# Hybrid attention block on one core: third-order step in the norms, one ring for V, norm weights on the keys, shorter merges

## The chip, the cores and the metric

The kernel runs on one core of a Trainium2 chip. The metric is the device time of one execution in microseconds, the median of the runs. The engines are TensorE (PE in the profile, PEld its weight loads), VectorE (DVE), ScalarE (ACT), GpSimd (POOL) and SyncE (SP, which issues most of the DMAs). Each engine works through its own instructions in the order in which they were written, and waits for other engines by semaphores.

## The reference, cut to what matters

```python
h = rms_norm(x, norm_gain)                       # x: 2048 tokens x 1024, float32
proj = h @ w_in                                  # q, k, v of A and B, SiLU gates, merge gates
# mixer A: 8 query heads, 2 key heads of 64, window 128 to both sides, sink logit
qa = rms_norm(qa, q_norm_a) / 8;  ka = rms_norm(ka, k_norm_a)
ya = banded_attention(qa, ka, va, bias, sink) * silu(ga)
# mixer B: 3 groups of 8 heads, dilation 1, 4, 16, window 64 neighbours to both sides
qb = rms_norm(qb, q_norm_b) / 8;  kb = rms_norm(kb, k_norm_b)
outs, lses = [dilated_group(qb[g], kb[g], vb[g], dilation[g]) for g in range(3)]
alpha = softmax(lses, over g)
yb = sum(alpha[g] * outs[g]) * silu(gb)
merged = sigmoid(gate_a) * (ya @ w_branch_a) + sigmoid(gate_b) * (yb @ w_branch_b)
y = x + merged @ w_out
```

The norm of a head divides 64 values by the root of their mean square and multiplies them by a weight per position in the head. In a logit the weight of q and the weight of k stand in one product, position by position, so the kernel multiplies them together beforehand (`GT`, one row of 64 for A and one for B) and applies the product on one side only.

## The kernel before, in words

Every matrix product is made with float16 pairs: a value is split into a high and a low half, and three of the four products are summed, so that the result is near float32.

**Start (to about 57 us).** x is loaded in 16 tiles of 128 tokens, squared on ACT, scaled by the inverse root of its mean square, transposed on PE and split into XH and XL (`x_square`, `x_stats`, `x_newton`, `x_scale`, `x_turn`, `x_hi`, `x_lo`). Tiles 0, 1 and tiles 2, 3 have their root on DVE (lines 277 to 279), the later groups of four on POOL (lines 272 to 275). The products of the first two gate columns run on PE from there on.

**Units (to about 1380 us).** 14 units of 8 steps each: 2 units of A and, for each of 4 pairs of heads, the B groups with dilation 4, 16 and 1. A step handles one `Pair`, two subsets of 128 tokens. `Pair.matmuls` (line 655) makes q, k and v of a subset in 24 products of 384 columns into one of two PSUM tiles `pj`. Then, per pair: ACT copies q and k out (`evac_qk`, 673), ACT and DVE take V out as a high and a low half into a tile `vt` (`v_hi` 688, `v_lo` 694), ACT squares q and k (701), DVE sums the squares and makes a first guess of the inverse root (706, 707, 263), POOL improves the guess with three Newton rounds of four instructions (`rs_newton`, 272 to 275), DVE multiplies q and k by the root (`scale`, 718), POOL multiplies q by the norm weights (`gain`, 725, two instructions), ACT and DVE split into halves (`hi` 731, `lo` 735), POOL makes a copy of k with the halves swapped (`swap`, 740), and a DMA transposes the result into a ring `kq` (`turn`, 748). For the dilated groups ACT copies an edge of the ring (758, 760). A PSUM tile `pj` is free again only when `v_lo` has read it.

Some steps later the attention items of these subsets follow: logits on PE (833), bias and maximum on DVE (848), exponentials on ACT (856), halves (861, 865), a transposing DMA (871), and the product with V on PE (`values`, 882). The tile `vt` has one extra column per head that holds 2^-14, so that the product also gives the denominator. POOL writes that column for every subset (`v_ones`, 681) into a tile from a pool of ten buffers (`vt`), or of four (`vw`) for the first subset of a dilated class, which is used again at its end.

The units of dilation 1 also merge the three groups, once for 256 tokens (`b_merge_q`): DVE takes the minimum over the groups and the differences (1023 to 1025), ACT the exponentials (1028), DVE the factors (1031 to 1036), POOL three products (1041), DVE the two sums (1047, 1048); later PE transposes the result (944). In these units every step has one merge. Gate products (`g_step`, line 310) fill some of the steps as a third block of matrix products in the two `pj` tiles.

**Order.** All engines' orders come from one list of events by time in steps: `at(time, function)` puts an event in, `until` takes events out while the matrix products are written. The constants say when: for a pair that ends at e, `NORM` puts the nine stages from square to turn at e + 0.028 ... e + 1.118, `EVAC` the copies at e + 0.015, 0.025 and 0.099, and `V_ONES` the column of ones at e - 0.077. On each engine a later event stands behind an earlier one, whether or not it needs it. An example is DVE, where `v_lo` of a pair's second subset stands behind `lo` of the pair before:

```python
NORM = (0.028, 0.136, 0.32, 0.626, 0.744, 0.904, 0.962, 1.033, 1.118)
EVAC = (0.015, 0.025, 0.099)
at(e[i] - V_ONES, self.v_ones, i)
```

**Tail (from about 1380 us).** The merge gates, the branch products and the output product, on PE almost without a pause; the change doesn't touch them.

Of the kernel before, what the change touches and what calls it, by code (L numbers as in the profile page):

```python
# [61 lines left out]

V_ONES = 0.077
EVAC = (0.015, 0.025, 0.099)
# [42 lines left out]
KQ_COPY = 0.45  # L107
VT_BUFS = 10
PT_BUFS = 4
# [4 lines left out]
def block_kernel(tc, x, w_units, w_gate, w_mrg, w_brn, w_out, w_bra, gain, qkg, sink, bias_a, bias_b, b_merge, out):  # L114
# [151 lines left out]
    def rs_newton(a, yv, r, n, pool):  # L266

        t = sm.tile([128, 10], F32, name="rs_t")
        tv = t[:, :n]
        for i in range(3):  # L270
            if pool:
                G.tensor_tensor(tv, yv, yv, OP.mult)  # L272
                G.tensor_tensor(tv, tv, a, OP.mult)  # L273
                G.tensor_scalar(tv, tv, -0.5, 1.5, OP.mult, OP.add)  # L274
                G.tensor_tensor(r if i == 2 else yv, tv, yv, OP.mult)  # L275
                continue
            V.tensor_tensor(tv, yv, yv, OP.mult)
            V.scalar_tensor_tensor(tv, tv, -0.5, a, OP.mult, OP.mult)
            V.scalar_tensor_tensor(r if i == 2 else yv, tv, 1.5, yv, OP.add, OP.mult)

# [302 lines left out]
    class Unit:  # L583


        def __init__(self, u):
            self.kind, self.idx, self.g = UNITS[u]
            self.u = u
            assert ("w", u) in done
            self.wh, self.wl = wtiles[u][3:5]  # L590
            if self.kind == "A":
                self.nq, self.nk, self.nv = 4, 1, 1
                self.d, self.n = 1, NT
            else:
                self.nq, self.nk, self.nv = 2, 2, 2
                self.d = DIL[self.g]
                self.n = S // self.d // 128
            self.br = 0 if self.kind == "A" else 1
            self.shift = self.kind == "B" and self.n > 1
            self.v, self.kq, self.t, self.done = {}, {}, {}, {}  # L600
            if self.kind == "A" or self.g == 0:
                self.nm = us.tile([128, NT, self.nq], F32, name=f"nm{self.kind}", bufs=2)

        def scales(self):
# [5 lines left out]
            V.tensor_scalar(self.eps[:], self.eps[:], EPS * QKE, None, OP.mult)  # L610
            self.wsc = ucol()
            V.tensor_scalar(self.wsc[:], inv[:], 2.0 ** 6 / SX, None, OP.mult)
            ws[UNITS[self.u]] = self.wsc

# [21 lines left out]
    ring = wk.tile([128, 6, 2 * RING], F16, name="kq", bufs=1)  # L636
    blocks = [0]

    class Pair:
# [34 lines left out]

        def v_ones(self, i):
            un, nv = self.un, self.un.nv
            if un.shift and self.subsets[i][1] == 0:
                vt = wk.tile([128, 2, 130], F16, name="vw", bufs=4)
            else:
                vt = wk.tile([128, 2, 130], F16, name="vt", bufs=VT_BUFS)  # L680
            G.memset(vt[:, :nv, HD:HD + 1], 2.0 ** -14)  # L681
            self.vt[i] = vt

        def v_hi(self, i):
            w = self.nh * HD
            nv, vt = self.un.nv, self.vt[i]
            psv = self.ps[i][:, w:w + nv * HD].rearrange("p (h e) -> p h e", e=HD)
            A.activation(vt[:, :nv, 0:HD], psv, AF.Copy, scale=VSC)
            self.vt[i] = vt, psv
# [30 lines left out]
        def gain(self):  # L720
            un, n = self.un, 2 * self.nh
            q = self.rw[:, :n * HD].rearrange("p (s h e) -> p s h e", s=2, e=HD)
            g = GT[un.br][:].unsqueeze(1).to_broadcast([128, un.nq, HD])
            for i in range(2):
                G.tensor_tensor(q[:, i, :un.nq, :], q[:, i, :un.nq, :], g, OP.mult)  # L725

# [43 lines left out]
    class Item:  # L770
# [103 lines left out]
        def values(self):  # L874
# [3 lines left out]
            for j in range(2):  # L878
                vh = 0 if un.kind == "A" else j
                for k, (p, c0, w) in enumerate(((self.ph, 0, HD + 1), (self.ph, 66, HD), (self.pl, 0, HD + 1))):  # L880
                    for s, key in enumerate(self.segs):
                        T.matmul(self.po[:, j, :w], lhsT=p[:, n * j + s, :], rhs=un.v[key][:, vh, c0:c0 + w],  # L882
                                 start=(k == 0 and s == 0), stop=(k == 2 and s == n - 1))

        def z_load(self):
# [123 lines left out]
    def b_merge_q(t, un, zz, q):  # L1009

        j = un.idx
        wscs = [ws[("B", j, g)] for g in range(3)]
        nm = zz[:, :, :, :, 65]
# [8 lines left out]
        def exponents():  # L1022
            V.tensor_tensor(mn[:], nm[:, 0], nm[:, 1], OP.min)
            V.tensor_tensor(mn[:], mn[:], nm[:, 2], OP.min)
            V.tensor_tensor(e[:], mn[:].unsqueeze(1).to_broadcast([128, 3, 2, 2]), nm, OP.subtract)
# [4 lines left out]
        def factors():  # L1030
            V.tensor_tensor(ed[:], e[:], den, OP.mult)
            V.tensor_tensor(sd[:], ed[:, 0], ed[:, 1], OP.add)
            V.tensor_tensor(sd[:], sd[:], ed[:, 2], OP.add)
            V.reciprocal(sd[:], sd[:])
            for g in range(3):
                V.scalar_tensor_tensor(e[:, g], e[:, g], wscs[g][:], sd[:], OP.mult, OP.mult)

# [53 lines left out]

    ws, fill = {}, {}
    for u in range(NU + 1):
# [684 lines left out]
```

## Time and profile before

| what | value |
|---|---|
| median of 3 runs | 1948.53 us (1947.81 to 1949.16) |
| the profiled execution, its own time | 1949.46 us |
| its span, first to last instruction | 1947.7 us |
| mean granted TensorE clock | 0.996 |
| PE busy, instructions | 1923.5 us, 99%, 13702 |
| DVE busy | 1373.0 us, 70%, 3604 |
| ACT busy | 1073.4 us, 55%, 2451 |
| POOL busy | 953.4 us, 49%, 2440 |

How to read it: matrix products are pipelined. One of 384 columns is shown with some 0.33 us, but one starts every 0.16 us, so the profile's busy time of PE says little about its pace; the distance from start to start says it. When PE waits, the profile shows the idle time behind the modelled end of the product before, which is 0.16 us later than the moment at which the next one could have started.

### The profile page before, as it was taken

The numbers are of one execution on the slowest core, as the hardware profiler recorded it, in microseconds if no ns is written. First come the engines' busy times: TensorE is split into PE (matmuls) and PEld (weight loads), VectorE is DVE, ScalarE is ACT, GpSimd is POOL, SyncE is SP. The second block draws the span as 40 slices with busy tenths as digits, with TensorE's granted clock in tenths as the row PEclk, the third lists the DMA queues.
The fourth block names the chain that finished last, engine by engine and source line by source line (L and its number), as shares of the span: only waits on it lengthen the run. The fifth ranks groups of instructions, "written<-read, shape, count | busy, mean of one in ns | idle before, by whom it ended". The sixth has DMA issues, their size and how long they took to land.

```text
span 1947.7 us, 40273 instructions
## 1 busy us (share of the span) xinstructions
PE 1923.5 (99%) x13702; PEld 1211.9 (62%) x13702; DVE 1373.0 (70%) x3604; ACT 1073.4 (55%) x2451; POOL 953.4 (49%) x2440
## 2 busy tenths in 40 slices
PE   7999999999999999999999999999999999999999
PEld 5556676677766688566787567876544444444444
DVE  6668787888767776677876878768776756876422
ACT  7457666776565566665666656666534545422100
POOL 4254456445546756647666676656511310232533
PEclk8999999999999999999999999999999999999999
DMA  6239977797858596677767776765822246778763
GB/s 252 82 75 174 192 154 158 137 188 147 189 96 189 117 189 124 127 147 163 159 130 147 138 173 123 144 120 115 187 82 96 99 157 202 217 236 269 248 243 140
DMA packets 589743, 307.96 MB, mean 158 GB/s; under 512 B 458081, under 2 KB 527329, under 8 KB 588257
## 3 DMA queue, kind: packets, MB, share of 16 engines
q1 hardware_dynamic: 571104, 296.73, 64.7%
q10 hardware_dynamic: 18432, 8.66, 1.9%
q8 instruction: 107, 1.75, 0.4%
q14 instruction: 100, 0.81, 0.1%
HBM read 129.91 MB, written 65.27 MB: 100 GB/s over the span
## 4 chain that ended last, share of the span: by engine, by line
PE 49%; DVE 4%; POOL 3%; issue 2%; ACT 1%; DMA 1%; SPq 0%; DVEq 0%; POOLq 0%
PE pj L655 16%; PE fps L310 13%; PE fps L1645 7%; PE pj L310 6%; PE fps L1440 5%; PE s L833 1%; PE pv L882 1%; POOL rs_t L272 1%; POOL rs_t L273 1%; DVE rw L718 1%; DVE qss L706 1%; POOL rs_t L274 1%; DMA kq<-spl 0%; POOL rs_y L275 0%; DVE pr L848 0%
## 5 line engine op out<-in xcount | busy, mean ns | idle before, releaser
L655 PE MATMUL pj<-wh,XH 128*128 128x384 f16 x1792 | 584.7, 326 | 6.2 <-DVE vt L694 6.2
L655 PE MATMUL pj<-wh,XL 128*128 128x384 f16 x1792 | 586.6, 327 | 0.0
L655 PE MATMUL pj<-wl,XH 128*128 128x384 f16 x1792 | 585.2, 327 | 0.0
L655 PEld LDWEIGHTS <-XH 128*128 128x128 f16 x3584 | 412.9, 117 | 155.1 <-issue 8.1
L848 DVE CUSTOM_DVE_ANT_0 pr<-s,b,ubuf 128x256 f32<-128x256 f32 (+3 forms) x512 | 218.4, 463 | 51.3 <-PE s L833 49.9
L655 PEld LDWEIGHTS <-XL 128*128 128x128 f16 x1792 | 207.8, 116 | 68.8 <-issue 0.2
L272 POOL TENSOR_TENSOR rs_t<-rs_y 128x8 f32<-128x8 f32 (+2 forms) x345 | 104.9, 304 | 211.9 <-DVE rs_y L263 153.1
L865 DVE SCALAR_TENSOR_TENSOR p<-pr,p 128x512 f16<-128x512 f32 (+2 forms) x256 | 185.9, 726 | 25.1 <-ACT p L861 24.2
L718 DVE TENSOR_TENSOR rw<-rw,qr 128x512 f32<-128x512 f32 (+1 forms) x112 | 110.8, 989 | 88.0 <-POOL vt L681 56.9
L725 POOL TENSOR_TENSOR rw<-rw,g 128x128 f32<-128x128 f32 (+1 forms) x224 | 128.9, 596 | 76.5 <-DVE rw L718 62.1
L310 PEld LDWEIGHTS <-wh 128*128 128x128 f16 x960 | 93.8, 98 | 111.4 <-issue 1.5
L861 ACT ACTIVATE p<-pr 128x512 f16<-128x512 f32 (+2 forms) x256 | 159.2, 622 | 6.3
L740 POOL COPY spl<-spl 128x256 f16<-128x256 f16 (+1 forms) x224 | 93.5, 447 | 130.4 <-DVE spl L735 128.9
L310 PE MATMUL fps<-Y,wh 128*128 128x512 f16 x512 | 152.3, 379 | 0.0
L833 PE MATMUL s<-kq 128*128 128x256 f16 (+3 forms) x1168 | 147.8, 254 | 2.0 <-ACT kq L758 2.0
L882 PEld LDWEIGHTS <-pt 128*128 128x128 f16 x3024 | 126.0, 98 | 35.0 <-issue 0.3
L310 PE MATMUL pj<-XH,gl 128*128 128x512 f16 x384 | 146.0, 380 | 0.0
L310 PE MATMUL pj<-XH,gh 128*128 128x512 f16 x384 | 146.0, 380 | 0.0
L310 PE MATMUL pj<-XL,gh 128*128 128x512 f16 x384 | 145.9, 380 | 0.0
L673 ACT ACTIVATE rw<-pj 128x256 f32<-128x256 f32 (+1 forms) x224 | 86.3, 385 | 107.8 <-PE pj L655 94.9
L1645 PE MATMUL fps<-wt,M 128*128 128x512 f16 (+1 forms) x684 | 145.2, 375 | 0.0
L731 ACT ACTIVATE spl<-rw 128x512 f16<-128x512 f32 (+1 forms) x112 | 72.1, 644 | 122.3 <-POOL vt L681 80.5
(245 smaller groups left out, 3679.9 us busy)
## 6 DMA issues: line engine op xcount, KB each, us to landing
wraw<-in_w_units_dram SPq DMA_DIRECT2D x56, 384.0 KB, 4.9
mtd<-mm SPq DMA_DIRECT2D x56, 256.0 KB, 3.8
M<-mtd SPq DMA_DIRECT2D x8, 1792.0 KB, 9.2
mgd<-fg SPq DMA_DIRECT2D x39, 256.0 KB, 2.1
zd<-z ACTq DMA_DIRECT2D x128, 66.0 KB, 2.5
zz<-zd SPq DMA_DIRECT2D x64, 132.0 KB, 2.8
xt<-in_x_dram SPq DMA_DIRECT2D x16, 512.0 KB, 8.6
gtd<-yo SPq DMA_DIRECT2D x32, 256.0 KB, 2.8
```

Source lines behind the costliest of these rows:

```text
L272: G.tensor_tensor(tv, yv, yv, OP.mult)
L310: out.append(lambda w=w, xx=xx, ch=ch, i=i: T.matmul(ps[:], lhsT=w[:, ch, c0:c0 + 128], rhs=xx[:, ch, ts], start=(i == 0), stop=(i == n - 1)))
L655: out.append(lambda lhs=lhs, rhs=rhs, ch=ch, k=k: T.matmul(ps[:, :384], lhsT=lhs[:, ch, :], rhs=rhs[:, ch, :], start=(k == 0), stop=(k == ...
L718: V.tensor_tensor(q, q, self.rr[:, :n].unsqueeze(2).to_broadcast([128, n, HD]), OP.mult)
L725: G.tensor_tensor(q[:, i, :un.nq, :], q[:, i, :un.nq, :], g, OP.mult)
L833: T.matmul(self.sv[j][:, o:o + k1 - k0], lhsT=q[:, h, qo:qo + 128], rhs=kt[:, un.nq + kh + v * un.nk, k0:k1], start=(v == 0), stop=(v == 1))
L848: V.tensor_tensor_reduce(out=self.pv[:, j, self.p0:self.p0 + W], in0=self.sv[j], in1=un.bias[:, self.h0 + j, self.b0:self.b0 + W], scale=I ...
L861: A.activation(self.sp[:, :128 * n], self.pr, AF.Copy, scale=PSC)
L865: V.scalar_tensor_tensor(self.sp[:, 128 * n:], self.pr, PSC, self.sp[:, :128 * n], OP.mult, OP.subtract)
L882: T.matmul(self.po[:, j, :w], lhsT=p[:, n * j + s, :], rhs=un.v[key][:, vh, c0:c0 + w], start=(k == 0 and s == 0), stop=(k == 2 and s == n ...
L1440: mm.append(lambda ch=ch, k=k, w=w, i=i: T.matmul(ps[:], lhsT=weight(bl, ch)[w], rhs=xblock(x, ch)[k], start=(i == 0), stop=(i == 11)))
L1645: mm.append(lambda ch=ch, k=k, w=w, i=i: T.matmul(ps[:, :cols.stop - cols.start], lhsT=m[:, a, ch, k, :], rhs=wt[w][:, b, ch, cols], start ...
```

## The change

Four things change.

1. **Third-order step.** `rs_newton` makes one step of third order (six instructions on POOL, four on DVE) and one Newton round (four on POOL, three on DVE) in place of three Newton rounds: ten instructions for twelve on POOL, seven for nine on DVE.
2. **Ring for V.** `vt` and `vw` become one tile of 14 slots. The column of ones is written once for all slots, ahead of the units. `v_hi` takes the slot that has been free longest, and a slot is given back where the last of the products that read it is written. `v_ones` is gone.
3. **Norm weights on the keys.** `gain` multiplies the keys of both subsets in one instruction (128 x 256 values in B, 128 x 128 in A), before the queries in two (of 128 x 128 in B, 128 x 256 in A).
4. **Merges.** The minimum and the sum over the three groups become one reduction each, and the three factors two instructions over all groups; the per-group scales that they need stand side by side in `wb`.

```diff
-        for i in range(3):
-            if pool:
-                G.tensor_tensor(tv, yv, yv, OP.mult)
-                G.tensor_tensor(tv, tv, a, OP.mult)
-                G.tensor_scalar(tv, tv, -0.5, 1.5, OP.mult, OP.add)
-                G.tensor_tensor(r if i == 2 else yv, tv, yv, OP.mult)
-                continue
...
+        if pool:
+            G.tensor_tensor(tv, yv, yv, OP.mult)
+            G.tensor_tensor(tv, tv, a, OP.mult)
+            G.tensor_scalar(r, tv, 0.375, -1.25, OP.mult, OP.add)
+            G.tensor_tensor(r, r, tv, OP.mult)
+            G.tensor_scalar(r, r, 1.875, None, OP.add)
+            G.tensor_tensor(yv, r, yv, OP.mult)
+            G.tensor_tensor(tv, yv, yv, OP.mult)
+            G.tensor_tensor(tv, tv, a, OP.mult)
+            G.tensor_scalar(tv, tv, -0.5, 1.5, OP.mult, OP.add)
+            G.tensor_tensor(r, tv, yv, OP.mult)
+            return
...
+            self.slot, self.uses = {}, {}
+            for i in range(self.n):
+                for r in range(self.d):
+                    self.uses[r, i] = 2 * (3 - (i in (0, self.n - 1))) if self.kind == "A" else min(self.n, 2)
...
+    vring = wk.tile([128, V_SLOTS, 2, 130], F16, name="vt", bufs=1)
+    vfree = list(range(V_SLOTS))
+    G.memset(vring[:, :, :, HD:HD + 1], 2.0 ** -14)
...
-                at(e[i] - V_ONES, self.v_ones, i)
...
-            nv, vt = self.un.nv, self.vt[i]
+            nv = self.un.nv
+            k = vfree.pop(0)
+            vt = vring[:, k]
+            self.un.slot[self.subsets[i]] = k
...
-            g = GT[un.br][:].unsqueeze(1).to_broadcast([128, un.nq, HD])
-            for i in range(2):
-                G.tensor_tensor(q[:, i, :un.nq, :], q[:, i, :un.nq, :], g, OP.mult)
+            k = q[:, :, un.nq:, :]
+            G.tensor_tensor(k, k, GT[un.br][:].unsqueeze(1).unsqueeze(1).to_broadcast([128, 2, un.nk, HD]), OP.mult)
...
+            for r, c in self.segs:
+                un.uses[r, c] -= 1
+                if not un.uses[r, c]:
+                    vfree.append(un.slot[r, c])
...
-            V.tensor_tensor(mn[:], nm[:, 0], nm[:, 1], OP.min)
-            V.tensor_tensor(mn[:], mn[:], nm[:, 2], OP.min)
+            V.tensor_reduce(mn[:], nm.rearrange("p g b h -> p b h g"), AX.X, OP.min)
...
-            V.tensor_tensor(sd[:], ed[:, 0], ed[:, 1], OP.add)
-            V.tensor_tensor(sd[:], sd[:], ed[:, 2], OP.add)
+            V.tensor_reduce(sd[:], ed[:].rearrange("p g b h -> p b h g"), AX.X, OP.add)
             V.reciprocal(sd[:], sd[:])
-            for g in range(3):
-                V.scalar_tensor_tensor(e[:, g], e[:, g], wscs[g][:], sd[:], OP.mult, OP.mult)
+            V.tensor_tensor(e[:], e[:], wscs, OP.mult)
+            V.tensor_tensor(e[:], e[:], sd[:].unsqueeze(1).to_broadcast([128, 3, 2, 2]), OP.mult)
```

The orders of PE, ACT and SP hold the same instructions at the same places before and after; only tile names and the semaphores waited for differ. Three places show what moves on the others and what ACT waits for.

POOL before, in the third unit of dilation 1 (around 1105 us of the trace): the last four rows of a pair's Newton rounds, a merge's products, the norm weights, and the columns of ones in between (`rs_t`, `rs_y`, `qr` hold the root, `zz` a merge, `rw` q and k, `wraw` weights, `spl` the halves).

```order
L275 TENSOR_TENSOR rs_y<-rs_t,rs_y 128x8
L272 TENSOR_TENSOR rs_t<-rs_y 128x8
L273 TENSOR_TENSOR rs_t<-rs_t,qss 128x8
L274 TENSOR_SCALAR rs_t<-rs_t 128x8
L275 TENSOR_TENSOR qr<-rs_t,rs_y 128x8
L1041 TENSOR_TENSOR zz<-zz,bm_e 128x4x64 x3
L681 MEMSET vt 128x2
L1020 COPY zz<-nmB 128x4
L725 TENSOR_TENSOR rw<-rw,g_874 128x128 x2
L326 TENSOR_TENSOR wraw<-wraw,gn 128x512
L681 MEMSET vt 128x2
L326 TENSOR_TENSOR wraw<-wraw,gn 128x512
```

The same place of POOL with the change, from the last six rows of the ten.

```order
L274 TENSOR_SCALAR qr<-qr 128x8
L275 TENSOR_TENSOR rs_y<-qr,rs_y 128x8
L276 TENSOR_TENSOR rs_t<-rs_y 128x8
L277 TENSOR_TENSOR rs_t<-rs_t,qss 128x8
L278 TENSOR_SCALAR rs_t<-rs_t 128x8
L279 TENSOR_TENSOR qr<-rs_t,rs_y 128x8
L1055 TENSOR_TENSOR zz<-zz,bm_e 128x4x64 x3
L1036 COPY zz<-nmB 128x4
L737 TENSOR_TENSOR rw<-rw,g_864 128x2x128
L334 TENSOR_TENSOR wraw<-wraw,gn 128x512 x2
```

Both `MEMSET` rows are gone, one `rw` row stands for two, and the rows ahead of `zz` are two fewer.

DVE before, a little later in the same unit: from the root's product with q and k (`rw`) over a merge's sums (`ya`) to the next merge's minimum and differences (`bm_n`, `bm_e`) and an item's maximum.

```order
L718 TENSOR_TENSOR rw<-rw,qr 128x512
L865 SCALAR_TENSOR_TENSOR p_17528<-pr,p_17528 128x512
L1047 TENSOR_TENSOR ya<-zz 128x256
L1048 TENSOR_TENSOR ya<-ya,zz 128x256
L1023 TENSOR_TENSOR bm_n<-zz 128x4
L1024 TENSOR_TENSOR bm_n<-bm_n,zz 128x4
L1025 TENSOR_TENSOR bm_e<-bm_n,zz 128x12
L848 ISA pr,nmB<-s,b_16506,ubuf 128x256
```

The same place of DVE with the change.

```order
L731 TENSOR_TENSOR rw<-rw,qr 128x512
L877 SCALAR_TENSOR_TENSOR p_16866<-pr,p_16866 128x512
L1061 TENSOR_TENSOR ya<-zz 128x256
L1062 TENSOR_TENSOR ya<-ya,zz 128x256
L1039 TENSOR_REDUCE bm_n<-zz 128x4
L1040 TENSOR_TENSOR bm_e<-bm_n,zz 128x12
L860 ISA pr,nmB<-s,b_15893,ubuf 128x256
```

One row is gone here; in the factors of the same merge two more go.

ACT before, in the first unit of A, with what each row waits for: the copy of q and k, then V's high half into a buffer of `vt`.

```order
L238 ACTIVATE wh<-wraw,ubuf 128x768
L673 ACTIVATE rw<-pj 128x320 [waits PE_49]
L688 ACTIVATE vt<-pj 128x64 [waits PE_49]
L701 ACTIVATE spl<-rw 128x640 [waits DMAHW2_49,DMAHW1_49,Activation_49]
L861 ACTIVATE p_1905<-pr 128x768 [waits DMAHW0_49]
```

The same rows with the change.

```order
L237 ACTIVATE wh<-wraw,ubuf 128x768
L692 ACTIVATE rw<-pj 128x320 [waits PE_49]
L701 ACTIVATE vt<-pj 128x64
L714 ACTIVATE spl<-rw 128x640 [waits DMAHW2_49,DMAHW1_49,Activation_49]
L873 ACTIVATE p_1858<-pr 128x768 [waits DMAHW0_49]
```

V's high half has no wait for PE of its own any more. Before, 9 of these 224 rows have one; with the change none has.

More of the change, by code (lines that the diff above doesn't have):

```diff
@@ L61 @@
 NPAIR = 8 * NU
-V_ONES = 0.077
 EVAC = (0.015, 0.025, 0.099)
@@ L107 @@
 KQ_COPY = 0.45
-VT_BUFS = 10
+V_SLOTS = 14
 PT_BUFS = 4
@@ L610, in scales @@
             V.tensor_scalar(self.eps[:], self.eps[:], EPS * QKE, None, OP.mult)
-            self.wsc = ucol()
+            if self.kind == "A":
+                self.wsc = ucol()
+            else:
+                if self.idx not in wb:
+                    wb[self.idx] = ubuf[:, ucount[0]:ucount[0] + 3]
+                    ucount[0] += 3
+                self.wsc = wb[self.idx][:, self.g:self.g + 1]
             V.tensor_scalar(self.wsc[:], inv[:], 2.0 ** 6 / SX, None, OP.mult)
-            ws[UNITS[self.u]] = self.wsc
         def bias_load(self):
@@ L1011, in b_merge_q @@
         j = un.idx
-        wscs = [ws[("B", j, g)] for g in range(3)]
+        wscs = wb[j].unsqueeze(2).unsqueeze(3).to_broadcast([128, 3, 2, 2])
         nm = zz[:, :, :, :, 65]
```

20 lines of the change are left out of this document (8 added, 12 removed).

## The prediction

> **What bounds the kernel now.** I read the page's engine shares first, then PE's part of the chain of waits, then who keeps PE waiting, and last the timeline around each of these waits.
>
> ```profile
> PE 1923.5 (99%) x13702; PEld 1211.9 (62%) x13702; DVE 1373.0 (70%) x3604; ACT 1073.4 (55%) x2451; POOL 953.4 (49%) x2440
> 1052.82 2.60 PE pj L655 x16
> PE s L470 <- DVE xt L464: 7.4, 3, 4.8
> PE pj L655 <- DVE vt L694: 6.2, 6, 2.0
> PE s L833 <- ACT kq L758: 2.0, 3, 1.2
> PE pt L944 <- DVE ya L1048: 0.7, 1, 0.7
> ```
>
> PE bounds it: 16 products in 2.60 us are one per 0.16 us, and the order of its instructions is the same after the change. So a shorter list on POOL (49% busy) or DVE (70%) is worth only what it takes out of PE's waits. The last four rows are those that POOL or DVE can shorten: 7.4 us at the start and 8.9 us in the units, in ten waits. Here are the ten:
>
> ```profile
> 101.47 0.32 PE L655 MATMUL pj<-wh,XH 128*128 128x384 f16 x1 [0.37 <-DVE vt L694]
> 875.47 0.32 PE L655 MATMUL pj<-wh,XH 128*128 128x384 f16 x1 [0.33 <-DVE vt L694]
> 1071.48 0.32 PE L655 MATMUL pj<-wh,XH 128*128 128x384 f16 x1 [0.52 <-DVE vt L694]
> 1085.39 0.62 PE L833 MATMUL s<-kq 128*128 128x128 f16 x8 [1.20 <-ACT kq L758]
> 1104.83 0.62 PE L833 MATMUL s<-kq 128*128 128x128 f16 x8 [0.46 <-ACT kq L758]
> 1112.95 0.32 PE L655 MATMUL pj<-wh,XH 128*128 128x384 f16 x1 [1.99 <-DVE vt L694]
> 1125.33 0.32 PE L655 MATMUL pj<-wh,XH 128*128 128x384 f16 x1 [1.05 <-DVE vt L694]
> 1360.06 0.32 PE L655 MATMUL pj<-wh,XH 128*128 128x384 f16 x1 [1.91 <-DVE vt L694]
> 1369.14 0.44 PE L944 MATMUL pt<-idf,ya 128*128 128x128 f32 x2 [0.68 <-DVE ya L1048]
> 1377.40 0.62 PE L833 MATMUL s<-kq 128*128 128x128 f16 x8 [0.34 <-ACT kq L758]
> ```
>
> A product is shown with 0.32 us but could be followed after 0.16, so each wait costs 0.16 us more than its idle time: 8.85 + 10 x 0.16 = 10.45 us. A long wait costs more. PE was busy for 1.43 us of the first stretch below, and the granted clock of the next is 0.51; that is 3.40 x 0.49 = 1.7 us. The same happens at the start (1.47 us busy, then 0.51).
>
> ```profile
> 24.65:28.05 3.40, 1.47 (x13) 1.06 (x11) 2.41 (x3) 1.17 (x4) 1.68 (x5) 1.00 1.03 391
> 28.05:31.45 3.40, 3.40 (x14) 1.96 (x13) 2.24 (x10) 3.25 (x7) 0.00 (x0) 0.51 1.03 401
> 1110.08:1113.50 3.42, 1.43 (x10) 0.74 (x9) 3.37 (x9) 2.53 (x8) 1.91 (x5) 1.00 0.67 142
> 1113.50:1116.90 3.40, 3.40 (x24) 2.31 (x23) 3.11 (x15) 3.14 (x9) 2.20 (x9) 0.51 1.09 101
> ```
>
> [...]
>
> Why is `vt` late? DVE's rows ahead of the longest wait:
>
> ```profile
> 1105.30 1.08 DVE L718 TENSOR_TENSOR rw<-rw,qr 128x512 f32<-128x512 f32 x1 [1.07 <-POOL qr L275]
> 1109.27 0.96 DVE L1024 TENSOR_TENSOR bm_n<-bm_n,zz 128x4 f32<-128x4 f32 x1
> 1110.26 1.02 DVE L1025 TENSOR_TENSOR bm_e<-bm_n,zz 128x12 f32<-128x12 f32 x1
> 1112.01 0.68 DVE L735 TENSOR_TENSOR spl<-rw,spl 128x512 f16<-128x512 f32 x1
> 1112.62 0.28 DVE L694 SCALAR_TENSOR_TENSOR vt<-pj,vt 128x128 f16<-128x128 f32 x1
> ```
>
> L694 itself is short. It stands behind L735 of the pair before, which needs ACT's half, which needs POOL's gain, which needs L718, which waited 1.07 us for POOL's root. The edges `kq` and the sums `ya` hang on the same root.
>
> **The change part by part.** *Newton.* The first and the last of twelve rows of one pair:
>
> ```profile
> 1114.04 0.20 POOL L272 TENSOR_TENSOR rs_t<-rs_y 128x8 f32<-128x8 f32 x1 [0.54 <-DVE bm_d L1031]
> 1117.64 0.20 POOL L275 TENSOR_TENSOR qr<-rs_t,rs_y 128x8 f32<-128x8 f32 x1
> ```
>
> Twelve take 3.80 us, 0.32 each in a serial chain; two fewer are 0.63 us earlier for every pair.
>
> *Gain.* Means by shape:
>
> ```profile
> L725 POOL TENSOR_TENSOR rw<-rw,g 128x128 f32<-128x128 f32 x192 | 104.0, 562 | 60.6 <-DVE rw L718 49.0 <-DVE bm_d L1031 5.6 <-DVE am_n L984 3.4
> L725 POOL TENSOR_TENSOR rw<-rw,g 128x256 f32<-128x256 f32 x32 | 24.9, 798 | 15.9 <-DVE rw L718 13.1 <-DVE am_n L984 2.0 <-DVE vt L694 0.8
> L1041 POOL TENSOR_TENSOR zz<-zz,bm_e 128x256 f32<-128x256 f32 x96 | 76.5, 823 | 27.8 <-DVE bm_e L1036 27.6 <-ACT wl L221 0.2
> ```
>
> In B two of 128x128 (1.12 us) become one of 256 values; L1041 is the same shape, 0.82. That is 0.30 us earlier. In A 2 x 0.80 become one of 128 values, 0.56: 1.04 earlier.
>
> *Ones and ring.* The memsets waited for the product with V that still read the buffer:
>
> ```profile
> POOL vt L681 <- PE pv L882: 58.0, 14, 7.8
> ACT vt L688 <- PE pv L882: 17.7, 9, 2.7
> ```
>
> 58 us of POOL's waiting and 17.7 of ACT's end, but none of PE's ten waits names them: POOL (`swap` and the next unit's weights) and ACT (the next evacuation) stood still while PE had work. I count nothing for them. Should that cover be wrong, it is a gain. The one memset of all slots is written at the units' start, where POOL has nothing else due. The new order gives no V copy a wait for PE, because the evacuation ahead of it already waits for a later product than the slot's last reader; so the ring adds none.
>
> *Merges.* A reduction that reads 12 values is not in the trace. Around it:
>
> ```profile
> L203 DVE TENSOR_REDUCE wm<-pt 128x1 f32<-128x4 f32 x18 | 2.8, 155 | 2.8 <-PE pt L196 2.7
> L706 DVE TENSOR_REDUCE qss<-spl 128x8 f32<-128x512 f32 x96 | 65.3, 680 | 7.7 <-ACT spl L701 6.6
> L1024 DVE TENSOR_TENSOR bm_n<-bm_n,zz 128x4 f32<-128x4 f32 x32 | 6.9, 215 | 1.3 <-DMA zz<-zd 0.2
> ```
>
> Between 0.16 and 0.68 us; I take 0.16, since 12 values are nearest to 4. Each reduction replaces two instructions of about 0.22, so it saves 0.28 or at the other end loses 0.24. Only the minimum lies on the path to L694, and between POOL's instructions such a row also took 0.96 us. I take 0.2 us.
>
> *The sum.* The root comes 0.63 us earlier, the gain 0.3, the minimum 0.2: about 1.1 us for a wait. Each wait loses the smaller of this and its length: 0.53 + 0.49 + 0.68 + 1.1 + 0.62 + 1.1 + 1.1 + 1.1 + 0.84 + 0.50 = 8.1 us. What is late next is the same chain one pair on: a PE that waited less at 1112 reaches 1125 sooner, and so after 1071 and 1360. In these steps without a gate product the chain stays the longer one; I give back 1.5 us, an estimate. That leaves 6.6. The wait at 1112 becomes 0.9 us of idle, so the clock stays up: 1.7 us.
>
> At the start there are two places:
>
> ```profile
> L277 DVE TENSOR_TENSOR rs_t<-rs_y 128x2 f32<-128x2 f32 x6 | 1.0, 161 | 0.2
> 10.18 1.94 PE L470 MATMUL s<-idf,xt 128*128 128x128 f32 x8 [4.79 <-DVE xt L464]
> 13.04 0.58 ACT L473 ACTIVATE XH<-s 128x512 f16<-128x512 f32 x1
> 25.64 1.49 DVE L464 TENSOR_SCALAR xt<-xt,xr 128x1024 f32<-128x1024 f32 x1 [1.72 <-POOL xr L275]
> 27.27 0.63 PE L470 MATMUL s<-idf,xt 128*128 128x128 f32 x4 [1.93 <-DVE xt L464]
> ```
>
> Two DVE rows fewer (0.16 each) bring the first transpose forward by 0.3 us, but ACT takes its result at 13.04, behind its own squares: nothing. In the second, DVE waited for POOL's root, and two rows fewer shorten it by 0.6. The wait of 1.93 becomes 1.3; whether the half clock behind it then goes depends on where the stretch falls, so I count half of 1.7, 0.9.
>
> Together 6.6 + 1.7 + 0.6 + 0.9 = 9.8 us. The profiled execution took 1949.46 us (span 1947.7), 0.93 over the median of 1948.53. The sum starts from it: 1949.5 - 9.8 = 1939.7, which is 8.8 under the median.
>
> **The rivals.** *All of it goes* (chance 0.15). If lateness doesn't carry over and gain and reduction save up to a microsecond more where DVE and POOL slow each other (L1024's 0.96 for 0.215), all ten waits end, with both half clocks and the 0.6 + 0.3 at the start: 10.45 + 3.4 + 0.9 = 14.8 us, 1934.7.
>
> *The waits come back* (0.12). If 0.5 us of the 1.1 arrives, DVE being busy with other rows at the time, the ten lose 0.49 + 9 x 0.5 = 5.0, less 1.5 given back, and both half clocks stay: 1949.5 - 3.5 = 1946.0, no change that counts. For it speaks that L718's wait is only 1.07 us of the seven between it and L694; against it that L694 follows that row in order.
>
> *The reductions are dear* (0.05). [...] As a mechanism here: at L706's 0.68 the minimum would lose 0.24 instead of saving 0.2, 0.44 at five waits in the merges; 2.2 us back, 1941.9.
>
> *Slower* (0.04). POOL's 14 waits for old V buffers could move to ACT's V copy if a slot were given back too early for its turn. Then ACT holds up the evacuation. A half of a pair is 24 products, 3.9 us, and the other `pj` tile covers that much; the longest wait, 7.8 us, would stop PE for 3.9. Fourteen such would cost 55 us, 1994.7; from four on (1939.7 + 15.6 = 1955.3) it is slower than before by more than the bound below. The mean of the 14 is 4.1 and costs 0.2, and the new order shows no such wait, so nearly nothing speaks for it.
>
> **How the numbers follow.** The forecast keeps 0.64; it is 1939.7. The range has to reach the waits' return on one side and their end on the other: 1934.5 to 1946.0, which leaves out the slower case and the outer halves of the two ends. A difference of 0.2%, 3.9 us, is about what a measurement of this kernel can tell from none; under 1944.6 is faster. The forecast, the full gain and the dear reductions are faster, 0.84; the return is the same, 0.12; slower 0.04.
>
> **What would show it.** Right: PE's wait for `vt` falls from 6.2 us to 2 or less, that for `kq` to under 1; ten POOL rows from first to `qr` in about 3.2 us; no wait of ACT or POOL for V's readers; the granted clock at full after 1100 us. Wrong: waits of PE for `vt` as long as before, or at other places, with the root earlier; a reduction of 0.5 us; the wait at 27 us unchanged.

## The result, and the profile after

The changed kernel takes 1935.38 us (median of 6 runs, 1935.14 to 1935.87); the kernel before took 1948.17 beside it (6 runs, 1945.95 to 1949.51). The ratio is 0.9935, 95% interval 0.9922 to 0.9948: 12.8 us less. The profiled execution took 1935.41 us with a span of 1933.6.

First the page's engine shares of the changed kernel.

```profile
PE 1920.1 (99%) x13702; PEld 1211.1 (63%) x13702; DVE 1353.2 (70%) x3504; ACT 1076.7 (56%) x2451; POOL 840.9 (43%) x1875
```

Then PE's waits (waited for: us in total, times, longest).

```profile
PE s L478 <- DVE xt L472: 4.6, 3, 3.4
PE pj L675 <- DVE vt L707: 0.8, 1, 0.8
```

PE issues the same 13702 products. Of 6.2 us of waiting for `vt`, 0.8 is left; the rows for the edges `kq` and for the sums `ya` are gone. Next, what stands at the place of the longest wait of before: from the root's product with q and k to `vt` on DVE, and POOL's rows beside it.

```profile
1096.67 1.08 DVE L731 TENSOR_TENSOR rw<-rw,qr 128x512 f32<-128x512 f32 x1 [0.52 <-POOL qr L279]
1100.46 0.16 DVE L1039 TENSOR_REDUCE bm_n<-zz 128x4 f32<-128x12 f32 x1
1100.66 0.81 DVE L1040 TENSOR_TENSOR bm_e<-bm_n,zz 128x12 f32<-128x12 f32 x1
1101.40 0.47 DVE L860 CUSTOM_DVE_ANT_0 pr<-s,b,ubuf 128x256 f32<-128x256 f32 x1
1102.91 0.28 DVE L707 SCALAR_TENSOR_TENSOR vt<-pj,vt 128x128 f16<-128x128 f32 x1
...
1096.59 2.65 POOL L1055 TENSOR_TENSOR zz<-zz,bm_e 128x256 f32<-128x256 f32 x3
1099.54 0.72 POOL L737 TENSOR_TENSOR rw<-rw,g 128x256 f32<-128x256 f32 x1
1100.22 2.21 POOL L334 TENSOR_TENSOR wraw<-wraw,gn 128x512 f32<-128x512 f32 x2
```

DVE waits 0.52 us for the root where it waited 1.07, and from there to `vt` it needs 1102.91 - 1096.67 = 6.24 us where it needed 1112.62 - 1105.30 = 7.32. Between the two rows DVE never pauses for more than 0.11 us at a time, before or after, so its own rows set `vt` there, not POOL's gain or ACT's half.

The clock, in stretches of the changed kernel (us; busy time and instructions of PE, PEld, DVE, ACT, POOL; granted clock; DMA share; GB/s):

```profile
24.26:27.67 3.41, 3.41 (x18) 2.46 (x17) 2.22 (x4) 1.85 (x5) 1.96 (x6) 0.53 0.99 386
1106.50:1109.90 3.40, 3.40 (x34) 2.38 (x33) 2.38 (x10) 2.81 (x7) 3.15 (x9) 1.00 0.70 149
1109.90:1113.30 3.40, 3.40 (x33) 2.54 (x32) 3.26 (x10) 2.87 (x7) 0.52 (x1) 1.00 0.84 184
```

In the units it stays full throughout, 1.00 from 80 to 1380 us. At the start a half clock is still there (0.53), some 4 us earlier than in the profiled execution of before.

PE's products can be matched one to one in the two traces. The lead, by which a product starts earlier after the change, grows at these places ("others" are waits that the forecast did not count):

| product of before, us | waited for, before | lead of after behind it, us | gained there |
|---|---|---|---|
| first of the units, 81.43 | x tiles, half clock | 1.59 | 1.59 |
| 101.47 | vt | 2.12 | 0.53 |
| 289.55, 508.38, 781.59 | others | 3.00 | 0.88 |
| 875.47 | vt | 3.51 | 0.51 |
| 1071.48 | vt | 4.19 | 0.68 |
| 1085.39 | kq | 5.67 | 1.48 |
| 1104.83 | kq | 6.31 | 0.64 |
| 1112.95 | vt | 8.47 | 2.16 |
| 1113.92 to 1117.03 | half clock | 10.10 | 1.63 |
| 1125.33 | vt | 10.32 | 0.22 |
| 1360.06 | vt | 12.40 | 2.08 |
| 1369.14 | ya | 13.27 | 0.87 |
| 1372.43 | others | 13.53 | 0.26 |
| 1377.40 | kq | 14.04 | 0.51 |

The ten places give 9.7 us, the half clock 1.6. The one wait that is left, before the product that stood at 1125.33, is at 1115.00 now.

### The profile page after: what moved, and what is told of

The parts are those of the page before. It is cut to its first block, busy times and chain, and to the rows that moved or that the text cites. A ratio compares the mean times of both kernels' runs of the same rounds, so it can differ in the third digit from the quotient of the medians.

```text
span 1933.6 us, 39422 instructions
## 1 busy us (share of the span) xinstructions
PE 1920.1 (99%) x13702; PEld 1211.1 (63%) x13702; DVE 1353.2 (70%) x3504; ACT 1076.7 (56%) x2451; POOL 840.9 (43%) x1875
## 4 chain that ended last, share of the span: by engine, by line
PE 93%; DVE 3%; DMA 1%; issue 1%; POOL 1%; ACT 1%; SPq 0%; ACTq 0%; DVEq 0%; POOLq 0%
PE pj L675 42%; PE pj L318 15%; PE fps L318 13%; PE fps L1659 8%; PE s L845 5%; PE fps L1454 5%; PE pv L894 4%; PE pt L960 1%; PE s L478 1%; DMA xt<-in_x_dram 0%; DVE rw L731 0%; DVE qss L719 0%; DVE p L877 0%; DMA wraw<-in_w_bra_dram 0%; PE pt L195 0%
## 5 line engine op out<-in xcount | busy, mean ns | idle before, releaser
L270 POOL TENSOR_TENSOR rs_t<-rs_y 128x8 f32<-128x8 f32 (+2 forms) x115 | 40.6, 353 | 254.0 <-DVE rs_y L262 199.8
L737 POOL TENSOR_TENSOR rw<-rw,g 128x256 f32<-128x256 f32 (+1 forms) x112 | 89.0, 794 | 124.5 <-DVE rw L731 82.9
L894 PE MATMUL pv<-vt,pt 128*128 128x65 f16 (+1 forms) x3024 | 132.6, 192 | 0.0
L181 POOL TENSOR_TENSOR wraw<-wraw,gn 128x768 f32<-128x768 f32 (+1 forms) x80 | 110.5, 1388 | 43.3 <-DMA wraw<-in_w_mrg_dram 43.3
```

What stands on the lines that cost most here:

```text
L181: G.tensor_tensor(v, v, gn[:, c0:c0 + 2].unsqueeze(2).to_broadcast([128, 2, n]), OP.mult)
L737: G.tensor_tensor(k, k, GT[un.br][:].unsqueeze(1).unsqueeze(1).to_broadcast([128, 2, un.nk, HD]), OP.mult)
```

## The experiments

The theory: PE waits where the chain from root to `vt` and `kq` is late, so what shortens POOL's root or DVE's rows behind it gains, and the parts act on the same waits. First rival (the ring theory): the ring, because POOL and ACT no longer stand behind the product with V. Second rival: each part has gains of its own that add up. Third rival (the load theory): POOL's busy time counts, because it slows DVE. Each ratio is to the kernel before on the same chip.

| kernel | median us | before us | ratio, 95% interval |
|---|---|---|---|
| only Newton | 1938.32 | 1949.61 | 0.9943 (0.9930 to 0.9955) |
| only ring | 1950.39 | 1949.61 | 1.0003 (0.9994 to 1.0012) |
| only gain | 1946.32 | 1949.61 | 0.9985 (0.9976 to 0.9994) |
| only merges | 1943.96 | 1949.61 | 0.9971 (0.9960 to 0.9983) |
| all but Newton | 1942.47 | 1948.67 | 0.9966 (0.9954 to 0.9979) |
| all but ring | 1935.55 | 1948.67 | 0.9930 (0.9917 to 0.9942) |
| all but gain | 1934.49 | 1948.67 | 0.9925 (0.9912 to 0.9937) |
| all but merges | 1939.37 | 1948.67 | 0.9950 (0.9937 to 0.9964) |
| only the minimum | 1943.02 | 1948.91 | 0.9971 (0.9961 to 0.9982) |
| low halves late, in before | 1959.95 | 1948.91 | 1.0055 (1.0043 to 1.0068) |
| low halves late, in after | 1935.64 | 1948.91 | 0.9932 (0.9919 to 0.9944) |
| a Newton round more, in after | 1967.18 | 1948.91 | 1.0097 (1.0083 to 1.0111) |

### One part alone

**Newton.** The kernel before with the new `rs_newton`.

```diff
-        for i in range(3):
...
+            G.tensor_scalar(r, tv, 0.375, -1.25, OP.mult, OP.add)
...
```

> The kernel before with the third-order step alone (ten POOL rows per pair for twelve). Chain theory (PE's waits end when the root comes earlier): each of the ten waits loses the smaller of 0.63 us and its length, 5.9 us, and the half clock after 1100 us may go: 1941 to 1943, PE's wait for V's tile falls from 6.2 us to about 3. Ring theory (what counts is that POOL no longer stands still behind V's readers): under 2 us of gain, 1946.5 to 1948. Load theory (what counts is POOL's busy time, which slows DVE): POOL loses some 50 us of its 953, about four tenths of the whole change's 112 us: 1943 to 1944.

It took 11.3 us off, to 1938.32, below the 1941 to 1943 that the theory of the chain gave when it let each wait lose 0.63 us at most. PE's wait for `vt`:

```profile
PE pj L664 <- DVE vt L703: 2.8, 3, 2.1
```

DVE's rows of two pairs that follow one another, at the place of before's 1112.95:

```profile
1088.91 0.69 DVE L727 TENSOR_TENSOR rw<-rw,qr 128x512 f32<-128x512 f32 x1 [0.20 <-POOL vt L690]
1098.19 1.08 DVE L727 TENSOR_TENSOR rw<-rw,qr 128x512 f32<-128x512 f32 x1 [0.53 <-POOL qr L280]
1102.16 0.96 DVE L1033 TENSOR_TENSOR bm_n<-bm_n,zz 128x4 f32<-128x4 f32 x1
1105.51 0.28 DVE L703 SCALAR_TENSOR_TENSOR vt<-pj,vt 128x128 f16<-128x128 f32 x1
```

The row of before that answers to the first of them (the one for the second, with 1.07, is in the prediction):

```profile
1095.48 0.69 DVE L718 TENSOR_TENSOR rw<-rw,qr 128x512 f32<-128x512 f32 x1 [0.79 <-POOL vt L681]
```

The wait for the root fell from 0.79 to 0.20 in the one pair and from 1.07 to 0.53 in the next. From root to `vt` DVE needs 7.32 us as before, since the rows of the merge are as long. Yet PE's start-to-start loss there fell from 2.15 us to 0.47, by 1.7. In this stretch DVE pauses for little but the root, so what two rows of POOL save in one pair, some 0.55 us, is still there in the next, and is added to: in seven pairs in a row, from 1056 to 1118 us, the product with the root (L718, here L727) starts 4.34, 4.88, 5.42, 5.97, 6.57, 7.11 and 7.65 us earlier than in before. The longest wait that is left, 2.06 us, is that of before's 1125.33 (1.05 there): PE reaches it sooner.

**Ring.** The kernel before with the slots.

```diff
-                at(e[i] - V_ONES, self.v_ones, i)
...
+            k = vfree.pop(0)
+            vt = vring[:, k]
```

> The kernel before with the ring for V alone: the waits of POOL (58.0 us in 14) and ACT (17.7 us in 9) for V's readers go, everything else stays. Chain theory: the root comes when it came, 1947.5 to 1949, PE's ten waits as before. Ring theory: most of the 12.8 us, 1937 to 1941. Load theory: 22 us less of POOL, about a fifth: 1945.5 to 1946.5.

```profile
PE pj L661 <- DVE vt L693: 6.7, 6, 2.4
PE s L832 <- ACT kq L757: 1.9, 3, 0.8
```

No gain (0.8 us slower, and the interval includes 1): PE's waits are about those of before, though POOL's and ACT's waits for these `vt` buffers are gone. DVE's total wait before the product with the root moves little:

```profile
L717 DVE TENSOR_TENSOR rw<-rw,qr 128x512 f32<-128x512 f32 (+1 forms) x112 | 106.5, 951 | 80.1 <-POOL qr L274 79.4
```

It was 88.0 before, most of it under the name of the memset that stood right behind the root on POOL. The first rival falls.

**Gain.** The kernel before with the weights on the keys.

```diff
-            for i in range(2):
-                G.tensor_tensor(q[:, i, :un.nq, :], q[:, i, :un.nq, :], g, OP.mult)
+            k = q[:, :, un.nq:, :]
+            G.tensor_tensor(k, k, GT[un.br][:].unsqueeze(1).unsqueeze(1).to_broadcast([128, 2, un.nk, HD]), OP.mult)
```

> The kernel before with the norm weights on the keys alone (one POOL row of 256 values per pair in B for two of 128, one of 128 in A for two of 256). Chain theory: 0.3 us earlier for each of nine waits, the wait at 101 us in the first unit of A gone: 3 us, 1945 to 1946. Ring theory: nothing, 1948. Load theory: 40 us less of POOL, about a third: 1944 to 1945.

```profile
PE pj L655 <- DVE vt L694: 5.1, 5, 2.0
```

3.3 us, with the longest wait as long as before. PE's wait for `kq` fell from 2.0 us to 0.8, that for `vt` from 6.2 to 5.1: the one of before's 1360.06 from 1.91 to 0.75, while those at 101.47 and 1071.48 are gone and two others are longer by 0.24 and 0.48.

**Merges.** The kernel before with the reductions and the two factors.

```diff
-            V.tensor_tensor(mn[:], nm[:, 0], nm[:, 1], OP.min)
-            V.tensor_tensor(mn[:], mn[:], nm[:, 2], OP.min)
+            V.tensor_reduce(mn[:], nm.rearrange("p g b h -> p b h g"), AX.X, OP.min)
...
+            V.tensor_tensor(e[:], e[:], wscs, OP.mult)
```

> The kernel before with the shorter merges alone (three DVE rows fewer per merge, two reductions of 12 values). Chain theory: only waits in the units with merges change, six at 875 us and after 1104 us, each by 0.2 to 0.8 us: 1.5 to 4 us with no half clock changed, 1944.5 to 1947. Ring theory and load theory: nothing, 1948 (POOL does the same as before). If the reductions are dear (0.5 us or more each): 1949 to 1951.

5.6 us, more than the 1.5 to 4 that were expected, and more than the forecast's 0.2 us at each of five waits. POOL does the same work here as before, so the third rival, by which this kernel gains nothing, falls. PE's wait for `vt` fell to 2.8 us in three places, and that at before's 1112.95 is gone with its half clock; the 1.9 that is left is that of before's 1125.33. `kq` is as before.

```profile
PE pj L660 <- DVE vt L699: 2.8, 3, 1.9
PE s L838 <- ACT kq L763: 2.1, 3, 1.2
```

### One part undone

These are the changed kernel with one part as it was before. For Newton:

```diff
-            G.tensor_scalar(r, tv, 0.375, -1.25, OP.mult, OP.add)
...
+        for i in range(3):
```

> The changed kernel with the three Newton rounds back. Chain theory (the parts shorten one chain, and what is left of PE's waits limits what they can save together): gain and merges alone gave 0.9985 and 0.9971 of the time before, some 8.5 us together, so 1939 to 1941, 4 to 6 us over the changed kernel; PE's waits for V's tile and the edges together 2 to 4 us. If the parts act each on waits of its own: 11 us over it, 1946.

For the ring:

```diff
+                at(e[i] - V_ONES, self.v_ones, i)
...
-            k = vfree.pop(0)
```

> The changed kernel with the old buffers for V and their columns of ones. Chain theory: as the changed kernel, 1935 to 1936.5. Ring theory in its weaker form (the ring only counts once the root is earlier, because then POOL and ACT stand first behind V's readers): 2 to 4 us over it, 1937.5 to 1939.5, with a wait of POOL for V's readers ahead of one of PE's.

For the gain:

```diff
-            G.tensor_tensor(k, k, GT[un.br][:].unsqueeze(1).unsqueeze(1).to_broadcast([128, 2, un.nk, HD]), OP.mult)
+                G.tensor_tensor(q[:, i, :un.nq, :], q[:, i, :un.nq, :], g, OP.mult)
```

> The changed kernel with the norm weights back on the queries, two instructions per pair. Chain theory: Newton and merges alone cover nearly all of PE's waits, so 1935.5 to 1937; the wait in the first unit of A (0.5 us) is back. If the parts act each on waits of its own: 2.9 us over the changed kernel, 1938.3.

For the merges:

```diff
-            V.tensor_reduce(mn[:], nm.rearrange("p g b h -> p b h g"), AX.X, OP.min)
+            V.tensor_tensor(mn[:], nm[:, 0], nm[:, 1], OP.min)
+            V.tensor_tensor(mn[:], mn[:], nm[:, 2], OP.min)
```

> The changed kernel with the old merges (two instructions each for minimum and sum, three for the factors). Chain theory: the third-order step alone left three waits of 2.8 us for V's tile, the longest of 2.1 us in the merges; with the gain's 0.3 us some 1 to 2 us over the changed kernel, 1936.5 to 1938. If the parts act each on waits of its own: 5.6 us over it, 1941.

Against the changed kernel's 1935.38, measured on another occasion, Newton undone costs 7.1 us by the medians (6.0 by the ratios to before) and the merges 4.0 (2.9); both cost more than the theory's 4 to 6 and 1 to 2 by the medians, and less than the 11 and 5.6 of parts that add up. Ring and gain undone cost nothing (0.2 more and 0.9 less). That PE's wait in the first unit of A would be back without the gain was wrong: its trace has no such wait. PE's wait for `vt`, in this order without Newton, without the merges, without the gain:

```profile
PE pj L666 <- DVE vt L698: 2.9, 2, 2.2
```

```profile
PE pj L670 <- DVE vt L702: 2.3, 1, 2.3
```

```profile
PE pj L675 <- DVE vt L707: 0.7, 1, 0.7
```

Alone, the four parts add up to 11.3 - 0.8 + 3.3 + 5.6 = 19.4 us; together they bring 12.8. The second rival falls: they shorten the same waits, and a wait can end only once. With the other three in, nothing is left for the gain.

### Only the minimum

Is it the number of rows in the merges, or which rows?

```diff
-            V.tensor_tensor(mn[:], nm[:, 0], nm[:, 1], OP.min)
-            V.tensor_tensor(mn[:], mn[:], nm[:, 2], OP.min)
+            V.tensor_reduce(mn[:], nm.rearrange("p g b h -> p b h g"), AX.X, OP.min)
```

> The kernel before with one edit: the minimum over the three groups is one reduction instead of two two-input rows; the sum and the factors stay. The four edits of the merges together brought 5.6 us. Theory of contention (a two-input row of a few values is held while POOL runs a long row, 0.96 us for 0.215 at the longest wait, and a reduction is not): the minimum alone brings most of it, with the wait at 1112 under 0.8 us and its half clock gone: 1949.6 becomes 1944 to 1946. Rival (plain price: 0.4 us of DVE rows become 0.16, at five of the waits): 0.24 x 5 = 1.2 us, the longest wait stays at 1.7 us and its half clock too: 1948.4. Rival (the sums and factors count as much): 1946.5 to 1947.5.

1943.02 us, ratio 0.9971: all of what the merges bring by themselves, 5.9 us here and 5.6 there. The sum and the factors bring nothing that can be measured. PE's wait at before's 1112.95 is gone with its half clock, and that at 1125.33 grew from 1.05 to 1.83 us. At the place of the longest wait, DVE's and POOL's rows of this kernel:

```profile
1102.35 1.08 DVE L718 TENSOR_TENSOR rw<-rw,qr 128x512 f32<-128x512 f32 x1 [1.05 <-POOL qr L275]
1105.31 0.64 DVE L1047 TENSOR_TENSOR ya<-ya,zz 128x256 f32<-128x256 f32 x1
1105.88 0.16 DVE L1023 TENSOR_REDUCE bm_n<-zz 128x4 f32<-128x12 f32 x1
1106.07 0.23 DVE L1024 TENSOR_TENSOR bm_e<-bm_n,zz 128x12 f32<-128x12 f32 x1
1106.22 0.47 DVE L848 CUSTOM_DVE_ANT_0 pr<-s,b,ubuf 128x256 f32<-128x256 f32 x1
...
1105.22 1.05 POOL L725 TENSOR_TENSOR rw<-rw,g 128x128 f32<-128x128 f32 x2
1106.23 1.03 POOL L326 TENSOR_TENSOR wraw<-wraw,gn 128x512 f32<-128x512 f32 x1
```

And the same stretch of before; its two rows L1024 and L1025 are in the prediction.

```profile
1108.82 0.41 DVE L1023 TENSOR_TENSOR bm_n<-zz 128x4 f32<-128x4 f32 x1
1111.20 0.47 DVE L848 CUSTOM_DVE_ANT_0 pr<-s,b,ubuf 128x256 f32<-128x256 f32 x1
...
1108.16 1.05 POOL L725 TENSOR_TENSOR rw<-rw,g 128x128 f32<-128x128 f32 x2
1109.17 1.04 POOL L326 TENSOR_TENSOR wraw<-wraw,gn 128x512 f32<-128x512 f32 x1
1110.21 1.04 POOL L326 TENSOR_TENSOR wraw<-wraw,gn 128x512 f32<-128x512 f32 x1
```

The wait for the root is the same (1.05 and 1.07). From L1023's start to L848's, before needs 1111.20 - 1108.82 = 2.38 us, this kernel 1106.22 - 1105.88 = 0.34. Before, L1023 ends at 1109.23, L1024 at 1110.23, L1025 at 1111.28; POOL's rows end at 1109.21, 1110.21 and 1111.25. Each of these small rows with two inputs ends 0.02 to 0.03 us after the POOL row beside it, and then meets the next. The reduction runs its 0.16 us under a POOL row that lasts on, and L1024 then stands only until that row's end, 0.23 us in all.

That holds for every such row of before and of the changed kernel. Of the six kinds of two-input rows in the merges of before (L1023 to L1025 and L1031 to L1033, 32 of each), 35 took over 0.3 us; all 35 ended 0.015 to 0.036 us after a POOL row of over 0.3 us, and none of the other 157 ran from start to end under such a row. In the changed kernel 17 two-input rows of the merges took over 0.3 us, all ending within 0.025 to 0.038 of a POOL row. Of its 64 reductions none took over 0.18, and six of them ran from start to end under such a POOL row.

### Low halves later in the order

The prediction's chain says that `vt` stands behind the low half of the pair before (L735). Here that half and the swapped copy come later, in both kernels; the DMA keeps its place and waits for them.

```diff
-NORM = (0.028, 0.136, 0.32, 0.626, 0.744, 0.904, 0.962, 1.033, 1.118)
+NORM = (0.028, 0.136, 0.32, 0.626, 0.744, 0.904, 1.1, 1.105, 1.118)
```

> The kernel before with one edit: the split into low halves, the swapped copy and the transposing DMA stand at 1.1, 1.105 and 1.118 instead of 0.962, 1.033 and 1.118, so that on DVE the low half of V stands ahead of the low half of q and k of the pair before. All work is the same. Theory of the order (vt is late only because its instruction stands behind lo): PE's six waits for vt (6.2 us, with 0.16 each 7.2) and the half clock behind the longest (1.7) go, at 6.7 to 8.9 us; lo itself is later by up to 0.14 of a step, some 1.6 us, so the waits for the edges kq may grow from 2.0 to up to 6.8; 1949 becomes 1940 to 1946, with vt below 1 us among PE's waits. Rival (vt is late of itself, by its PSUM tile, by ACT's high half or by DVE being busy with other rows): vt stays at 5 to 6 us and the time at 1948 to 1951.

> The changed kernel with the same edit: low halves, swapped copy and transposing DMA at 1.1, 1.105 and 1.118. All work is the same. One wait of PE for vt is left in the changed kernel, 0.8 us idle and 0.99 us from start to start. Theory of the order: it goes, 1935.4 becomes 1934.4. If the edges kq come late instead, they appear among PE's waits with 1 to 4 us: 1935.5 to 1938. Rival (vt is late of itself): the wait of 0.8 us stays, 1935.4.

PE's waits, first of before with the edit, then of after with it:

```profile
PE pj L655 <- DVE vt L694: 5.1, 7, 1.4
PE s L833 <- DMA kq<-spl: 4.4, 5, 1.5
PE s L833 <- ACT kq L758: 3.3, 3, 1.5
PE pv L882 <- DMA pt<-p: 2.0, 3, 1.1
```

```profile
PE pv L894 <- DMA pt<-p: 1.3, 4, 0.6
PE pj L675 <- DVE vt L707: 0.4, 1, 0.4
```

Before became slower by 11.0 us, outside of what either theory said. The waits for `vt` are seven instead of six, 5.1 us instead of 6.2, none over 1.4 us: the low half is 0.68 us of some seven that stand ahead of it. So the order of that one row alone isn't the cause. And keys that come later are waited for at once (4.4 us more for the transposing DMA). In the changed kernel the wait for `vt` is halved and four new ones for `pt` take its place: 1935.64 against 1935.38, no gain.

### A Newton round more

The changed kernel with 14 POOL rows instead of ten.

```diff
             G.tensor_scalar(tv, tv, -0.5, 1.5, OP.mult, OP.add)
+            G.tensor_tensor(yv, tv, yv, OP.mult)
+            G.tensor_tensor(tv, yv, yv, OP.mult)
+            G.tensor_tensor(tv, tv, a, OP.mult)
+            G.tensor_scalar(tv, tv, -0.5, 1.5, OP.mult, OP.add)
             G.tensor_tensor(r, tv, yv, OP.mult)
```

> The changed kernel with one Newton round more on POOL behind the two steps: 14 rows instead of ten, which makes the root of each pair about 1.27 us later than in the changed kernel and 0.63 later than before. It does more work than it needs. Theory of the chain with slack: the two rows of the earlier run without the new step cost 7.1 us; four rows reach more pairs and the half clock, so the cost is more than twice that, 14 to 25 us: 1949 to 1960, with vt and kq at 10 us or more among PE's waits. Rival (each of the ten places pays the rows' price and no other place does): 10 x 1.27 = 12.7 less the slack of those places, at most 1946. Rival (the place of the rows among POOL's other work is what counts, not their sum): no more than the 7.1 of two rows, 1942 to 1943.

PE's wait for `vt`, and the group of DVE's product with the root:

```profile
PE pj L679 <- DVE vt L711: 17.5, 18, 2.2
```

```profile
L735 DVE TENSOR_TENSOR rw<-rw,qr 128x512 f32<-128x512 f32 (+1 forms) x112 | 109.9, 981 | 150.0 <-POOL qr L283 149.8
```

It costs 31.8 us, above even the 14 to 25 us that the theory of the chain gave. Two rows more (Newton undone) cost 7.1, four cost 31.8, so the second two cost 24.7. PE waits for `vt` at 18 places instead of one, and DVE waits for the root 150.0 us in all; in the changed kernel that sum is 20.4:

```profile
L731 DVE TENSOR_TENSOR rw<-rw,qr 128x512 f32<-128x512 f32 (+1 forms) x112 | 103.1, 920 | 20.4 <-POOL qr L279 19.7
```

Both rivals, with at most 12.7 and 7.1 us, fall. The chain had slack for most pairs; past it, the lateness of one pair is the next one's too.

## Why the prediction came out as it did

The forecast was 1939.7 and the time is 1935.4: inside the range, faster as forecast, and closer to the rival in which all waits end (1934.7). The mechanism was right, its size too small: in the units 6.6 + 1.7 = 8.3 us was forecast, and some 12.5 came. The nearness to that rival's number bears out half of its reasons: rows of DVE that lasted until a POOL row ended (0.96 and 1.02 us at the longest wait, 0.215 and 0.233 in the mean) counted for much more than was summed, but lateness does carry over from pair to pair. By its steps:

- **PE bounds, and only its waits count.** Right. The ring took over 70 us of waiting from POOL and ACT and no time from the kernel, alone or undone, as the zero counted for it said.
- **Newton, 0.63 us for a pair.** Nearly right for the rows: from the first to the end of `qr`, ten take 3.27 us in the median of the 112 pairs and twelve 3.81, so 0.54. What failed is the use of it: "each wait loses the smaller of this and its length" has every wait gain from one pair alone. A pair's 0.55 adds to the next pair's; at 1112.95 Newton alone took 1.7 us.
- **"I give back 1.5 us."** It happened at one place only. At before's 1125.33, where 1.1 was counted, the whole change gains 0.22 and 0.99 us of start-to-start waiting is left; in five kernels with some of the parts (only Newton, only merges, only the minimum, all but Newton, all but merges) the wait there is 1.83 to 2.31 us, against 1.05 before.
- **Gain, 0.3 us.** The price holds: one row of 256 values takes 0.83 us in the mean, two of 128 took 1.12. But at the longest waits the gain isn't on the path from root to `vt`, where DVE doesn't pause for it. By itself it acts on `kq`, and from pair to pair: with the gain alone the lead of the product with the root grows from 2.35 to 3.50 us over nine pairs (before's 1254 to 1324 us). That makes 3.3 us by itself, and nothing on top of the rest.
- **The minimum, 0.2 us.** This term was mis-sized most, and it is the step that failed at the longest waits. The reduction took 0.16 us as assumed, but what it replaces was priced from means (0.243 and 0.215), with L1024's 0.96 noted beside it. At the longest waits the rows before needed 2.38 us, and the reduction takes 2.0 of it away in the kernel with the minimum alone. In the changed kernel, where L1040 still meets a POOL row (0.81 us), it is 2.38 - (1101.40 - 1100.46) = 1.4.
- **"The reductions are dear"** fell: mean 0.167 us for both, at no place over 0.18.

```profile
L1039 DVE TENSOR_REDUCE bm_n<-zz 128x4 f32<-128x12 f32 x32 | 5.4, 167 | 2.4 <-DMA zz<-zd 2.3
L1047 DVE TENSOR_REDUCE bm_s<-bm_d 128x4 f32<-128x12 f32 x32 | 5.3, 167 | 1.1
```

- **The sum at the ten waits.** 8.1 less 1.5 was forecast; 9.7 came, with 1.0 left at one place. Four other places that the forecast didn't count gave 1.1 more.
- **The half clock after 1112**, 1.7 us: right, 1.63.
- **The start, 1.5 us (0.6 and half of 1.7).** The first part was right as a step: two rows fewer on POOL bring DVE's wait for that root from 1.72 to 1.19 us, and in the changed kernel without the gain, where the clock is full at that time, PE's wait is 1.41 us instead of 1.93. In the profiled execution of the changed kernel the wait itself is gone, because a half clock just ahead of it (24.26 to 27.67, above) keeps PE busy until then:

```profile
27.24 0.62 PE L478 MATMUL s<-idf,xt 128*128 128x128 f32 x3
```

A half clock falls there both with and without the change: six of the 14 profiled executions have one between 23 and 32 us (before with 0.51, the changed kernel with 0.53, only Newton, all but ring, and both with late low halves), eight have none (only ring, with 1.00 from 20.85 to 34.5 us, is one). That the place of the stretch decides it, on which the forecast counted half of 1.7, was an estimate that no run shows. And the lead of 1.59 us is in the main luck. The first product of the units stands at 81.43 us in the profiled execution of before, but at 79.63 to 80.12 (mean 79.92) in the six others with three Newton rounds, and at 79.11 to 80.16 (mean 79.62) in the six with the new step of ten rows. By these the start gives some 0.3 us, less than its scatter.

So of the 14.05 us between the two profiled executions some 12.5 come from the units, and the 12.8 of the medians are that and little else.

The wait that is left belongs to a stretch in which DVE has a gate's weights to split as well:

```profile
1112.86 1.28 DVE L364 SCALAR_TENSOR_TENSOR gl<-wraw,ubuf,gh 128x1024 f16<-128x1024 f32 x1
1114.06 0.69 DVE L747 TENSOR_TENSOR spl<-rw,spl 128x512 f16<-128x512 f32 x1
1115.00 0.32 PE L675 MATMUL pj<-wh,XH 128*128 128x384 f16 x1 [0.83 <-DVE vt L707]
```

## What to carry to other kernels

Find the engine that never pauses between the late input and the wait, and count its rows at that place, not their means over the program: here a small two-input row of VectorE beside a long row of GpSimd lasted until that row ended, up to 1.02 us for a mean of 0.233, and a reduction took 0.16 there. Where the steps followed one another on such an engine, a saving in one added to the next, 0.54 to 0.60 us from pair to pair with Newton alone, and a loss grew in the same way: two small rows more in each pair cost some 7 us here, and four 32. Waiting that engines did off that chain, 70 us of it here, went without an effect on the time that could be measured (1950.39 us with the ring alone, 1949.61 before).

## What the runs showed of the hardware

- **VectorE and GpSimd.** Two-input rows of 4 or 12 values took 0.15 to 1.02 us in the merges of before, by where a GpSimd row beside them ended; reductions of 12 values took 0.16 to 0.18 us at all 64 places of the changed kernel.
- **The half clock.** A wait of PE of 2.31 us, longer than the 1.99 that stood ahead of half a clock in before, left it full in the changed kernel without the merges.

```profile
1116.84 0.32 PE L670 MATMUL pj<-wh,XH 128*128 128x384 f16 x1 [2.31 <-DVE vt L702]
```

The changes of the granted clock lie whole multiples of 3.41 us apart in the trace of before (28.14, 31.55, 1113.58 and 1116.99 us) and in that of the changed kernel (13.82, 24.06 and 27.47 us). Two stretches of that length that hold the wait of 2.31 us:

```profile
1111.83:1115.25 3.42, 2.70 (x28) 2.02 (x27) 3.25 (x11) 2.70 (x8) 0.24 (x1) 1.00 0.90 196
1115.25:1118.66 3.41, 1.82 (x13) 1.38 (x13) 3.20 (x11) 1.46 (x6) 1.30 (x5) 1.00 0.69 195
```

PE was busy for 2.70 and 1.82 us of them; in before it was busy for 1.43 us of the 3.42 ahead of the half clock at 1113.58. The busy time of PE alone doesn't tell the cases apart: at the start of the changed kernel 1.66 us from 20.64 to 24.05 stood ahead of half a clock, and with the ring alone 1.50 us stood ahead of a full one:

```profile
24.26:27.67 3.41, 1.50 (x14) 1.13 (x13) 1.72 (x2) 1.67 (x4) 2.15 (x7) 1.00 1.04 375
27.67:31.08 3.41, 3.41 (x24) 2.41 (x25) 3.04 (x11) 2.83 (x5) 0.00 (x0) 1.00 1.03 403
```

What sets off the half clock no run here shows.
